# Weight pages that begin at another place of a 128-byte line in each stage

## The chip, the cores and the metric

The kernel runs on one core of one Trainium2 chip. The metric is the device time of one execution in microseconds (us). The time before is the median of three runs, 1609.99 us, and they lie between 1606.26 and 1611.5 us.

## The reference, cut to what matters

One layer of an encoder block on a sequence of 1024 tokens with 1024 channels, all in float32. Nearly all of the arithmetic is matrix products with the weights:

```python
h = rms_norm(h_res, norm_w[layer])
z = jnp.einsum('bsd,dc->bsc', h, w_in[layer])            # 1024 x 1024 by 1024 x 12288
qkv_a, g_a, q_b, zf_fwd, zf_bwd, i_b, g_b, zgate_a, zgate_b = jnp.split(z, split_points, axis=-1)
...                                                      # banded attention, 3 groups of 8 heads
y_a = (o_a * silu(g_a)) @ w_proj_a                       # 512 x 1024
...                                                      # gated linear recurrence, 8 heads, two directions
y_b = o_b @ w_proj_b                                     # 1024 x 1024
merged = sigmoid(zgate_a) * y_a + sigmoid(zgate_b) * y_b
h_res = h_res + merged @ w_out                           # 1024 x 1024
```

## The kernel before, in words

A product in float32 is made of three products in the faster type float32r: each operand x is split into a rounded part and a remainder (names with `hi` and `lo`, `sh` and `sl`, `mh` and `ml`), and hi·hi, hi·lo and lo·hi are summed in PSUM. So each step of a large product is three matmuls, and each of them has a 128x128 operand that is loaded into the array first (the stationary one) and a 128x512 operand that streams through it (the moving one). 5520 matmuls have this size.

The weights come as pages of 128x512 (2048 bytes in each partition). `feed` loads a raw page, `split` writes its rounded part into a tile `whi` (ScalarE) and the remainder into a tile `wlo` (GpSimd, for 16 pages VectorE). Both come from rings of 9 tiles, `hir` and `lor`, and `free_to` gives the tiles back once the products of a page have been issued. All pages are numbered in the order in which they are used; `split_next` is the number of the page that is split next, `b.w[n]` holds the two tiles of page n.

The normed input h stands transposed in SBUF for most of the run, in the tiles `hhi` and `hlo`. There are two kinds of product with it:

- `tok_group`: the weight page is moving, 128 tokens of h are stationary. Values, queries and keys of the attention, and i and g of the recurrence (called ig below) are made so. In the attention groups 1 and 2 the tokens are taken with a stride.
- `T_group`: a 128x128 part of the weight page is stationary, 512 tokens of h are moving. The gates and the q, f and f-backward columns of the recurrence are made so.

`run_unit` runs a group: 8 steps of three matmuls, 24 matmuls, into one PSUM bank `gp`. `run_quads` makes most of the gate columns with seven products for eight (tiles `qA`, `qC`, `qE`, sums of h in the tiles S0 to S3).

The order of the work is decided while the program is built, by a planner (`Plan`, `Builder`) with modelled times: `tick` and `burst` place the smaller tasks (splits, evacuations, and the small float32 matmuls of attention and recurrence) between the large groups. Rings of tiles with a fixed count decide how far ahead a task may run: `qq_ring` holds the evacuated q of the recurrence, `ld` the branch outputs that are loaded back from HBM before the output projections (`split_load`, then `split_store` into `sh` and `sl`).

The stages in order, with the large matmuls in each: u and V0 (values of group 0; 192), qk0 (384), values and qk of groups 1 and 2 with strided tokens (1152), ga (gate of branch A; 192), ig (four parts of 192), quads (504), the eight recurrence heads (144 each), sg (the last gates; 192), ya (projection of branch A; 192), yb (branch B; 384), out (output projection; 384). Small float32 matmuls run between the large ones nearly everywhere from qk0 to the last head.

Where the tiles lie, counted in bytes from the start of a 128-byte line: in the program before, `whi`, `wlo`, `hhi`, `hlo`, the sums S0 to S3 and the tiles of branch B in yb all begin at 96. The tiles of the attention and of the recurrence, `uhi` and `ulo` (the stationary operands of u), the tiles `sh` and `sl` of branch A (moving in ya) and `mh` and `ml` (stationary in out) begin at 32. The pages follow each other at 2048 bytes.

Of the kernel before, what the change touches and what calls it, by code (L numbers as in the profile page):

```python
# [8 lines left out]
F32 = mybir.dt.float32  # L9
F32R = mybir.dt.float32r  # L10
# [199 lines left out]
class Builder:  # L210
# [89 lines left out]
    def setup_weights(self, items, pool, ring, raws):  # L300
        self.RING = ring
        self.wpages, self.windex, self.quads, self.steps = [], [], [], []
        n = 0
        for k, it in enumerate(items):
            if not isinstance(it, tuple):
                self.wpages.append(it)
                self.windex.append(n)
                n += 1
                continue
            m = len(self.quads)  # L310
            self.quads.append(it)
            more = k + 1 < len(items) and isinstance(items[k + 1], tuple)
            if k == 0 or not isinstance(items[k - 1], tuple):
                self.steps.append((n, m, "11"))
                n += 1
            for op in ("T1", "T2", "21", "T3", "+", "22", "T4"):
                if op != "+":
                    self.steps.append((n, m, op))
                    n += 1
                elif more:  # L320
                    self.steps.append((n, m + 1, "11"))
                    n += 1
        self.ops = n
        self.w = {}
        self.rawr = self.ring(pool, "raw", raws, [128, 512])
        self.hir = self.ring(pool, "whi", ring, [128, 512], F32R)
        self.lor = self.ring(pool, "wlo", ring, [128, 512], F32R)
        self.raws = []
        self.raw_next = 0
        self.split_next = 0  # L330
        self.freed = 0
        self.offered = None
        self.scales = {}
# [17 lines left out]
            self.offer(t, k)  # L351

    def split(self, raw):
        hi, lo = self.hir.get(), self.lor.get()
        scale = self.scales.get(self.split_next)
        if scale is None:
            self.p.act.activation(hi, raw, AF.Copy)
            self.p.pool.tensor_tensor(lo, raw, hi.bitcast(F32), op=OP.subtract)
        else:
            self.p.act.activation(hi, raw, AF.Copy, scale=scale)  # L360
            self.p.dve.scalar_tensor_tensor(lo, raw, scale, hi.bitcast(F32), op0=OP.mult, op1=OP.subtract)
        self.w[self.split_next] = (hi, lo)
        self.split_next += 1
# [10 lines left out]

    def free_to(self, n):
        for i in range(self.freed, n):
            hi, lo = self.w.pop(i)
            self.hir.done(hi)
            self.lor.done(lo)
        self.freed = max(self.freed, n)  # L380
# [184 lines left out]
def hybrid_block(ctx, tc, a, out):  # L565
    b = Builder(ctx, tc, a)
    a_, v_, g_, t_, s_ = b.p.act, b.p.dve, b.p.pool, b.p.pe, b.p.sp
    consts = ctx.enter_context(tc.tile_pool(name="consts", bufs=1))
    wpool = ctx.enter_context(tc.tile_pool(name="wts", bufs=1))
    stg = ctx.enter_context(tc.tile_pool(name="stg", bufs=3))  # L570
    tiny = ctx.enter_context(tc.tile_pool(name="tiny", bufs=2))
# [31 lines left out]
    blocks = [(0, j) for j in range(0, 8, 2)] + [(1, j) for j in range(0, TAIL, 2)]  # L603
# [7 lines left out]
        items += gate_pages(1, j)  # L611
    items += [wpa[i] for i in range(8)] + [wpb[i] for i in range(16)] + [wo[i] for i in range(16)]
    b.setup_weights(items, wpool, RING, RAWS)


    nw = consts.tile([128, 8], F32, name="nw")
# [694 lines left out]
    hp = bctx.enter_context(tc.tile_pool(name="hgrn", bufs=1))  # L1311
# [25 lines left out]

    ig_ring = b.ring(hp, "ig", 8, [128, 512])
    sk_ring = b.ring(hp, "sk", 5, [128, 512])
    qq_ring = b.ring(hp, "q", 3, [128, 512])  # L1340
    lf_ring = b.ring(hp, "lf", 4, [128, 512])
    q2_ring = b.ring(hp, "q2", 4, [128, 4, 64])
    km_ring = b.ring(hp, "km", 4, [128, 512])
# [307 lines left out]
    ectx = {}  # L1651

    def end_start():
        bctx.close()
        ectx["ep"] = ep = ctx.enter_context(tc.tile_pool(name="end", bufs=1))
        ectx["ld"] = b.ring(ep, "ld", 6, [128, 512])
        for k in range(8):
            b.task("sp", [oaD], lambda k=k: split_load(OA, k % 4, k // 4, oaD[k % 4, k // 4],
                                                       lambda n: ep.tile([128, 512], F32R, tag="L", name=n, bufs=17)),
                   4, ectx["ld"].soon)  # L1660

    def split_load(to, j, half, src, new):
        t = ectx["ld"].get()
        s_.dma_start(t, src)
        b.task("act", [t], lambda: split_store(to, j, half, t, new), 4)
# [9 lines left out]
    for j in range(TAIL, 8):  # L1675
        for half in range(2):
            b.run_unit([T_group(pos, half, evac_sg(1, j, half), half == 1)])
            if not ectx and all(st.get("f", 0) == 2 for st in H.values()):
                end_start()
        pos += 2  # L1680
    b.drain()
    if not ectx:
        end_start()
        b.drain()
# [6 lines left out]
    ep = ectx["ep"]  # L1691
    ob = ctx.enter_context(tc.tile_pool(name="endo", bufs=1, side="right"))
    MA, MH, ML = {}, {}, {}
    for half in range(2):
        for h in range(8):
            k = 8 * half + h
# [39 lines left out]
    k = 0  # L1736
# [137 lines left out]
def _build(arrays):  # L1874
    import concourse.bacc as _bacc
    nc = _bacc.Bacc("TRN2", target_bir_lowering=False, num_devices=1)
    args = {n: nc.dram_tensor(f"in_{n}_dram", v.shape, mybir.dt.from_np(v.dtype), kind="ExternalInput").ap()
            for n, v in arrays.items()}
    out = nc.dram_tensor("out_0_dram", (S, D), F32, kind="ExternalOutput").ap()
    with tile.TileContext(nc) as tc:  # L1880
        hybrid_block(tc, args, out)
    return nc
# [9 lines left out]
```

## Time and profile before

| what | value |
|---|---|
| median of the runs | 1609.99 us (1606.26 to 1611.5) |
| the profiled execution | 1608.46 us, its span 1606.6 us |
| granted TensorE clock, mean | 0.99 |
| TensorE busy | 1569.1 us, 98% of the span |
| VectorE, ScalarE, GpSimd busy | 845.3, 659.5, 468.0 us |
| DMA | 148.31 MB, mean 92 GB/s |

TensorE is the engine to look at: it is busy nearly all of the span, the others half of it or less. A busy TensorE still says little about its pace, since matmuls overlap and their recorded ends are modelled. The pace is read from the start times of matmuls that follow each other, in the order of time; that distance is called the spacing below.

### The profile page before, as it was taken

What the parts mean: (1) busy time and instruction counts of PE and PEld (TensorE: products, weight loads), DVE (VectorE), ACT (ScalarE), POOL (GpSimd) and SP (SyncE); (2) the same over time, 40 slices, a digit from 0 to 9 for tenths busy, and PEclk for the clock granted to TensorE, in tenths of its full rate; (3) what the DMA queues carried; (4) which work ended last, traced back from release to release, by engine and by line L of the source; (5) the groups of instructions that cost most, each with busy time, mean ns of one, the idle gap of its engine ahead of it and who ended that gap; (6) DMA issues with size and microseconds to landing.
All of it is one profiled execution on the core that took longest, in us unless ns stands there. A gap on an engine that the chain in (4) does not pass through costs nothing. (4 is left out here: it accounts for less than half of the span.)

```text
span 1606.6 us, 23188 instructions
## 1 busy us (share of the span) xinstructions
PE 1569.1 (98%) x8373; PEld 1335.8 (83%) x8373; DVE 845.3 (53%) x2216; ACT 659.5 (41%) x1434; POOL 468.0 (29%) x462
## 2 busy tenths in 40 slices
PE   8899999999999999999899999999999999999999
PEld 6688899999999987678788888888877878888887
DVE  5667632575136642336412207988889887543211
ACT  5533542434334363213334437655565554422110
POOL 3411202202022031228434434433344423003320
PEclk9999999999999999899999999999999999999999
DMA  6402203102022035473413251121221211842232
GB/s 215 139 22 98 70 18 112 50 33 67 21 63 66 16 103 138 125 219 112 144 66 115 83 166 40 53 93 40 54 86 47 94 39 65 293 140 92 88 119 89
DMA packets 110879, 148.31 MB, mean 92 GB/s; under 512 B 24625, under 2 KB 48300, under 8 KB 110764
## 3 DMA queue, kind: packets, MB, share of 16 engines
q1 hardware_dynamic: 103340, 146.38, 29.1%
q8 instruction: 66, 1.08, 0.3%
q10 hardware_dynamic: 7424, 0.45, 0.3%
q14 instruction: 49, 0.40, 0.1%
HBM read 110.77 MB, written 40.73 MB: 94 GB/s over the span
## 5 line engine op out<-in xcount | busy, mean ns | idle before, releaser
L55 POOL TENSOR_TENSOR wlo<-raw,whi 128x512 fp32r<-128x512 f32 x192 | 253.9, 1328 | 685.8 <-ACT whi L55 670.4
L55 PE MATMUL gp<-whi,hhi 128*128 128x512 f32 x792 | 328.5, 415 | 8.3 <-ACT stage L55 5.7
L55 PE MATMUL gp<-wlo,hhi 128*128 128x512 f32 x792 | 316.0, 399 | 1.4 <-POOL wlo L55 1.4
L55 PE MATMUL gp<-whi,hlo 128*128 128x512 f32 x792 | 316.1, 399 | 0.0
L55 PEld LDWEIGHTS gp<-whi,hhi 128*128 128x128 f32 x792 | 200.5, 253 | 36.8 <-issue 10.0
L55 PEld LDWEIGHTS gp<-wlo,hhi 128*128 128x128 f32 x792 | 201.4, 254 | 18.3 <-POOL wlo L55 2.6
L55 PEld LDWEIGHTS gp<-whi,hlo 128*128 128x128 f32 x792 | 200.9, 254 | 17.9 <-DVE hlo L55 1.0
L55 PE MATMUL gp<-hhi,whi 128*128 128x512 f32 x512 | 209.4, 409 | 0.0
L55 PE MATMUL gp<-hhi,wlo 128*128 128x512 f32 x512 | 200.9, 392 | 0.0
L55 PE MATMUL gp<-hlo,whi 128*128 128x512 f32 x512 | 200.0, 391 | 0.0
L55 ACT ACTIVATE whi<-raw 128x512 fp32r<-128x512 f32 x192 | 119.3, 626 | 140.9 <-PE gp L55 81.7
L55 PEld LDWEIGHTS gp<-hhi,wlo 128*128 128x128 f32 x512 | 96.2, 188 | 21.3
L55 PEld LDWEIGHTS gp<-hhi,whi 128*128 128x128 f32 x512 | 96.8, 189 | 18.8 <-issue 1.0
L55 PEld LDWEIGHTS gp<-hlo,whi 128*128 128x128 f32 x512 | 96.8, 189 | 17.2
L55 ACT ACTIVATE s<-s,neg 128x192 f32<-128x192 f32 (+2 forms) x192 | 83.9, 439 | 65.5 <-DVE neg L55 65.3
L55 DVE TENSOR_REDUCE ss<-sq 128x8 f32<-128x512 f32 x48 | 32.8, 684 | 146.7 <-ACT sq L55 146.7
L55 POOL TENSOR_TENSOR wlo<-qraw,whi 128x512 fp32r<-128x512 f32 x42 | 55.0, 1316 | 76.9 <-ACT whi L55 76.7
L55 PE MATMUL gp<-sh,whi 128*128 128x512 f32 x192 | 75.0, 391 | 0.0
L55 PE MATMUL gp<-sh,wlo 128*128 128x512 f32 x192 | 74.9, 390 | 0.0
L55 PE MATMUL gp<-sl,whi 128*128 128x512 f32 x192 | 74.6, 389 | 0.0
L55 ACT ACTIVATE sq<-gp 128x512 f32<-128x512 f32 x48 | 28.0, 592 | 111.8 <-PE gp L55 91.4
L55 ACT ACTIVATE stage<-gp 128x512 f32<-128x512 f32 x48 | 28.0, 594 | 111.5 <-PE gp L55 88.3
(225 smaller groups left out, 2787.9 us busy)
## 6 DMA issues: line engine op xcount, KB each, us to landing
raw<-in_w_in_dram SPq DMA_DIRECT2D x168, 256.0 KB
igD<-stage SPq DMA_DIRECT2D x32, 256.0 KB
ig<-igD SPq DMA_DIRECT2D x32, 256.0 KB
sgl<-sgD SPq DMA_DIRECT2D x32, 256.0 KB
oD<-os SPq DMA_DIRECT2D x48, 128.0 KB
og<-oD SPq DMA_DIRECT2D x24, 256.0 KB
qraw<-in_w_in_dram SPq DMA_DIRECT2D x24, 256.0 KB
sgD<-spare SPq DMA_DIRECT2D x24, 256.0 KB
```

What stands on the lines that cost most here:

```text
L55: got = f(*args, **kw)
```

## The change

Each page is split into a tile that is 32 elements (128 bytes) longer than the page, and begins at a place in it that a table `place` gives for the page's number. Two small tiles that nothing uses are put in front, so that the tiles begin at 64 within a line; with the table's offsets the places are 68, 72, 80, 88, 92, 100, 104, 112, 120 and 0, and 96 for pages that the table does not name. To make room in SBUF, `qq_ring` has 2 tiles instead of 3 and `ld` 5 instead of 6.

```diff
-        self.hir = self.ring(pool, "whi", ring, [128, 512], F32R)
-        self.lor = self.ring(pool, "wlo", ring, [128, 512], F32R)
+        self.hir = self.ring(pool, "whi", ring, [128, 544], F32R)
+        self.lor = self.ring(pool, "wlo", ring, [128, 544], F32R)
+        self.wt = {}
+        self.place = {}
...
     def split(self, raw):
-        hi, lo = self.hir.get(), self.lor.get()
+        self.wt[self.split_next] = self.hir.get(), self.lor.get()
+        o = self.place.get(self.split_next, 96)
+        o = (o - 64) // 4 if o else 16
+        hi, lo = (t[:, o:o + 512] for t in self.wt[self.split_next])
...
+    consts.tile([128, 8], F32, name="lowPad")
+    consts.tile([128, 16], F32, name="lowPad2")
...
+    first = 112 + 7 * len(blocks)
+    spans = [(8, 16, 104), (16, 24, 112), (80, 88, 120), (88, 96, 0), (96, 104, 88), (104, 112, 80), (72, 80, 92)]
+    spans += [(first + 6 * h, first + 6 * h + 6, o) for h, o in enumerate((104, 112, 120, 0, 88, 80, 72, 100))]
+    spans += [(first + 48, first + 56, 68)]
+    for lo, hi, o in spans:
+        b.place.update({k: o for k in range(lo, hi)})
...
-    qq_ring = b.ring(hp, "q", 3, [128, 512])
+    qq_ring = b.ring(hp, "q", 2, [128, 512])
...
-        ectx["ld"] = b.ring(ep, "ld", 6, [128, 512])
+        ectx["ld"] = b.ring(ep, "ld", 5, [128, 512])
```

By stage, with the weight page moving or stationary, and h (the other operand) at 96:

| stage | large matmuls | the weights are | their place |
|---|---|---|---|
| qk0, first half, second half | 192, 192 | moving | 104, 112 |
| ga | 192 | stationary | 92 |
| ig, parts 1 to 4 | 192 each | moving | 120, 0, 88, 80 |
| heads 0 to 7 | 144 each | stationary | 104, 112, 120, 0, 88, 80, 72, 100 |
| sg | 192 | stationary | 68 |

All others keep 96. The two small tiles in front move every other tile of that side of SBUF as well: in the program after, what began at 32 begins at 0 (the tiles of attention and recurrence, `uhi` and `ulo`, `sh` and `sl` of branch A, `mh` and `ml`), and what began at 64 begins at 32. The other side, with h, S0 to S3 and the tiles of branch B, stays at 96. The pages now follow each other at 2176 bytes, 17 lines.

TensorE's instructions stand in the same order as before, and so do GpSimd's. On SyncE, which issues the loads, the shorter ring moves one load of branch A behind a load of a weight page (`raw`) and a store of a gate (`sgD`), at the start of ya. Before:

```order
L55 DMA ld_13001<-oaD 128x512
L55 DMA ld_13003<-oaD 128x512
L55 DMA ld_13005<-oaD 128x512
L55 DMA ld_13007<-oaD 128x512
L55 DMA ld_13009<-oaD 128x512
L55 DMA ld_13011<-oaD 128x512
L55 DMA raw_13019<-in_w_proj_b_dram 128x512
L55 DMA sgD<-stage_13041 128x512
L55 DMA ld_13044<-oaD 128x512
L55 DMA ld_13046<-oaD 128x512
```

On SyncE at the same place after the change:

```order
L55 DMA ld_13003<-oaD 128x512
L55 DMA ld_13005<-oaD 128x512
L55 DMA ld_13007<-oaD 128x512
L55 DMA ld_13009<-oaD 128x512
L55 DMA ld_13011<-oaD 128x512
L55 DMA raw_13019<-in_w_proj_b_dram 128x512
L55 DMA sgD<-stage_13041 128x512
L55 DMA ld_13044<-oaD 128x512
L55 DMA ld_13046<-oaD 128x512
L55 DMA ld_13059<-oaD 128x512
```

Five loads instead of six stand ahead of the page, and three instead of two behind the store. Later in ya some of the 16 loads of branch B trade places with loads of gates in the same way, and with them a few of the ScalarE and VectorE instructions that split them.

On ScalarE the ring of q adds a wait for VectorE in heads 2, 4 and 6, where the first q of the head is evacuated. `on`, `km` and `qr` are tiles of the recurrence too. Before, in head 2:

```order
L55 ACTIVATE on_9819<-oB_9807 128x512 [waits PE_49]
L55 ACTIVATE q_9827<-gp_9777 128x512 [waits PE_49]
L55 ACTIVATE km_9850<-lf_9721 128x4x64 [waits DVE_49,Activation_49,Pool_49]
L55 ACTIVATE km_9850<-q_8_9799 128x4x64 [waits DVE_49]
L55 ACTIVATE qr_9853<-lf_9721 128x512
```

On ScalarE at the same place after the change:

```order
L55 ACTIVATE on_9821<-oB_9809 128x512 [waits PE_49]
L55 ACTIVATE q_9829<-gp_9779 128x512 [waits DVE_49,PE_49]
L55 ACTIVATE km_9852<-lf_9723 128x4x64 [waits DVE_49,Activation_49,Pool_49]
L55 ACTIVATE km_9852<-q_8_9801 128x4x64 [waits DVE_49]
L55 ACTIVATE qr_9855<-lf_9723 128x512
```

The row of q has `DVE_49` among its waits, and nothing else moved there.

More of the change, by code (lines that the diff above doesn't have):

```diff
@@ L376, in free_to @@
         for i in range(self.freed, n):
-            hi, lo = self.w.pop(i)
+            self.w.pop(i)
+            hi, lo = self.wt.pop(i)
             self.hir.done(hi)
```

## The prediction

> **What bounds the kernel now.** I read the page first, for the engine and the chain that ended last.
>
> ```profile
> PE 1569.1 (98%) x8373; PEld 1335.8 (83%) x8373; DVE 845.3 (53%) x2216; ACT 659.5 (41%) x1434; POOL 468.0 (29%) x462
> ...
> 1369.90 232.96 PE gp L55 x1014
> ```
>
> TensorE (PE) is busy for 98% of the span, and the chain that ended last is, for its final 233 us, nothing but large matmuls one behind the other. So the time is set by the pace of matmuls that never wait, and a change of their operands' places acts on the end directly. That pace is the spacing of starts, from the order of time. Three stages run without a break, so their first and last start and their count give it. First the fourth part of ig (192 matmuls, from 785.69 to the first matmul after it), then ya (192, from 1382.04 to 1426.00), then out (383 spacings, from 1513.09 to 1602.46):
>
> ```profile
> 785.69 0.39 PE L55 MATMUL gp<-whi,hhi 128*128 128x512 f32 x1
> 829.21 0.39 PE L55 MATMUL qA<-hhi,whi 128*128 128x512 f32 x1
> ...
> 1382.04 0.40 PE L55 MATMUL gp<-sh,whi 128*128 128x512 f32 x1
> 1426.00 0.40 PE L55 MATMUL gp<-sh,whi 128*128 128x512 f32 x1
> ...
> 1513.09 0.40 PE L55 MATMUL gp<-whi,mh 128*128 128x512 f32 x1
> 1602.46 0.39 PE L55 MATMUL gp<-whi,ml 128*128 128x512 f32 x1
> ```
>
> ig: 43.52 us / 192 = 226.7 ns. ya: 43.96 / 192 = 229.0 ns. out: 89.37 / 383 = 233.3 ns. The matmuls have one shape and type, the clock is full, no other instruction lies between. What differs is where the operands begin in a 128-byte line: both at 96 in ig, moving at 32 and stationary at 96 in ya, moving at 96 and stationary at 32 in out. So places do matter, by up to 6.7 ns, and the equal pair 96/96 is the fastest of the three.
>
> Where small matmuls interrupt the large ones, the spacing needs time to settle. After such a break in ga:
>
> ```profile
> 579.24 0.40 PE L55 MATMUL gp<-hlo,whi 128*128 128x512 f32 x1
> ...
> 579.94 0.39 PE L55 MATMUL gp<-hlo,whi 128*128 128x512 f32 x1
> 580.16 0.39 PE L55 MATMUL gp<-hhi,wlo 128*128 128x512 f32 x1
> ...
> 581.55 0.39 PE L55 MATMUL gp<-hhi,wlo 128*128 128x512 f32 x1
> 582.23 0.39 PE L55 MATMUL gp<-hhi,wlo 128*128 128x512 f32 x1
> ```
>
> Ten spacings, 579.24 to 581.55, take 2.31 us, 231 ns each, though every operand stands at 96; the next three, to 582.23, take 0.68 us, 227 ns. The same pair has thus a slower, unsettled pace and a settled one, and single spacings between are as short as 0.22 us (579.94 to 580.16).
>
> **The change part by part.** It moves 2688 large matmuls to another place: qk0 384, ga 192, ig 768, the heads 1152, sg 192. Nothing is added to TensorE, and nothing moves there. Not all of these spacings are free to change: ig (768) and head 0 (144) run nearly all settled, the other 1776 stand among small matmuls, and of a group of 24 about ten recover as above and one or two hold the break. I count half of them, 888. That makes 1800 spacings whose settled value the new place decides.
>
> No row shows the new pairs. The bounds from rows: above, out's 233.3 ns, 6.7 ns over the present 226.7; below, the shortest single spacing seen, 0.22 us, 6.7 ns under it. Times 1800 that is +12.1 us and -12.1 us. For the value I weigh two readings. If the spacing grows evenly with the distance between the two places, the nearest rows are ya and out, both 64 bytes apart, at 229.0 and 233.3, mean 231.2, 4.5 ns over. The new distances are 4 to 32 bytes, 17 on average over the moved matmuls, which gives 4.5 x 17/64 = 1.2 ns. If instead 96/96 is special and any other pair stays at an unsettled pace, the price is 231 - 226.7 = 4.3 ns. I take the middle, 2.8 ns, since the two rows at 64 lie on both sides of that pace: 1800 x 2.8 ns = +5.0 us.
>
> A second reading of the same three numbers is worth having: 226.7 and 233.3 are 34 and 35 times 6.67 ns, and 229.0 is 34 and a third. The spacing seems to snap to steps. Then single stages will stay exactly at 226.7, or go to 233.3, or lie at a fraction, and the sum is a mean over the stages; the 2.8 ns is that mean, not the price of each.
>
> The two pads move operands of stages that keep 96. In out (384) the stationary operand goes from 32 to 0: from 64 bytes apart to 32. Half way between 226.7 and 233.3 is 230.0, so 384 x -3.3 ns = -1.3 us, with ends -2.6 (226.7) and 0. In u (about 80 free spacings, the same pair) -0.3. In ya the moving operand goes from 32 to 0, again from 64 to 32 apart; its 229.0 lies between the other two already, so 0, with ends -0.4 (226.7) and +0.8 (233.3). The small matmuls have both operands moved by the same 32 bytes, so I cost them at nothing; were that wrong, the cover would be none, since they lie on TensorE's path.
>
> [...]
>
> The shorter rings. The first q of heads 2, 4 and 6 now waits until the head before has used its q up. The last use by head 1 and the first q of head 2:
>
> ```profile
> 1046.67 0.68 DVE L55 TENSOR_TENSOR qr<-qr,q 128x512 f32<-128x512 f32 x1
> ...
> 1062.68 0.60 ACT L55 ACTIVATE q<-gp 128x512 f32<-128x512 f32 x1 [0.78 <-PE gp L55]
> ```
>
> The tile is free at 1047.4 and wanted at 1062.7: 15 us of cover, cost 0. Behind that ScalarE instruction stand the exponentials of the neighbouring head, which would be late if the cover went. Of `ld`, the sixth load of branch A now waits for the first tile, and stands behind a page and a store:
>
> ```profile
> 1378.54 2.06 DVE L55 TENSOR_TENSOR sl<-ld,sh 128x512 fp32r<-128x512 f32 x3 [0.71 <-ACT sh L55]
> ...
> 1384.19 1.28 DVE L55 TENSOR_TENSOR sl<-ld,sh 128x512 fp32r<-128x512 f32 x2
> ...
> 1413.07 0.68 DVE L55 TENSOR_TENSOR sl<-ld,sh 128x512 fp32r<-128x512 f32 x1
> ```
>
> Before, branch A's last two tiles are ready at 1385.5. A group of ya has four steps, 12 matmuls; the second starts 12 spacings after 1382.04, at 1384.8, and needs the last tile nine spacings on, at 1386.9. The eighth load now waits for the third tile's split, which ended at about 1379.9, and could come some 1 to 2 us later than before against a cover of 1.4 us: I cost it at 0, at most 1 us once, and the second group of ya would show it. Branch B's last split ends at 1413.8 and yb begins at 1426.0, 12 us of cover. SyncE's loads of pages behind it are taken in by the raw ring.
>
> Sum: +5.0 - 1.3 - 0.3 = +3.4 us on the profiled execution's 1608.5, 1611.9. That execution is 1.5 us under the median, 1610.0, so I predict 1613.4. A difference under 0.3%, 4.8 us, is about what a measurement of this kernel cannot tell from none.
>
> **The rivals.** *Slower by more:* most new pairs lock at the pace of out. Its place is the settled part of ig and the heads; +12.1 us, with out unchanged, gives 1622. It decides from a mean price of 3.6 ns on (1800 x 3.6 = 6.5 us, less 1.6, is 4.9), a mean spacing of 230.3. For it: two of the three pairs seen are slower, and 96/96 is the only one that settles at 34 steps. A second sign: ya and out are both 64 bytes apart and differ by 4.3 ns, so the distance within a line is not all that counts; pages at 17 lines now alternate between even and odd lines, and if that matters quads and yb (888 matmuls at 226.7 now) lose too, half of them up to 6.7 ns, 3 us. Against it: most new pairs are nearer to each other than 64.
>
> *Faster:* equal places are no good place for two streams that start together, and some new ones settle below 226.7. It decides from -1.8 ns, 224.9 (1800 x -1.8 = -3.2 us, less 1.6, is -4.8). At the lower bound 1610 - 12.1 - 2.9 = 1595; half way, about 1602. For it: single spacings of 0.22 us occur. Against it: no stage holds one, and both other pairs seen are slower.
>
> *Nothing happens:* the places of these pairs make no difference, as between equal pairs, and only noise is left: 1610. [...] For it: if the spacing snaps to steps, a small shift may leave a stage on its step. Against it: it would have to hold for ten places at once.
>
> **How the numbers follow.** Forecast (a small loss inside 0.3%) 0.34, nothing happens 0.07, a loss over 0.3% 0.40 of which about half in the neighbourhood of the forecast and half towards 1622, faster 0.19. So faster 0.19, same 0.41, slower 0.40. The forecast's own range is 1608 to 1616. The range given reaches up to 1623, the upper rival with its time, and down to 1602, the middle of the lower one; beyond are about 2 in 10.
>
> **What would show it.** The starts of the large matmuls, stage by stage: the four parts of ig one by one, head 0, and after each break whether the spacing comes back to 226.7. I expect them between 226.7 and 233.3, unequal among the places, with a mean near 229.5; out under 233.3; quads and yb still at 226.7; no new wait of TensorE at the start of ya or in heads 2, 4 and 6. The prediction is wrong if the places change nothing, if most stages lock at 233 or above, or if any of them settles near 220.

## The result, and the profile after

The change makes the kernel slower: 1621.14 us median (1620.77 to 1622.49) against 1609.7 us of the kernel before, a ratio of 1.0075 with a 95% interval of 1.0057 to 1.0093. The time lies inside the range given, near its upper end. It is the value of the rival "slower by more" (1622), not of the forecast (1613.4).

The page of the kernel after, with its profiled execution of 1622.49 us, and the last and longest piece of its chain of work:

```profile
span 1620.7 us, 23188 instructions
...
PE 1588.1 (98%) x8373; PEld 1340.7 (83%) x8373; DVE 835.6 (52%) x2216; ACT 659.9 (41%) x1434; POOL 457.3 (28%) x462
```

```profile
1380.84 236.08 PE gp L55 x1014
```

The span grew by 14.1 us, with the same 8373 matmuls and TensorE still busy for 98% of it. The same 1014 matmuls at the end of the chain take 236.08 us instead of 232.96. So the time went into the pace of the matmuls, which the order of time gives. First one row of before that the prediction did not need, the first matmul after the quads, then the rows of after: the fourth part of ig, the quads, the first head, ya, yb and the two ends of out.

```profile
943.45 0.39 PE L55 MATMUL gp<-hhi,whi 128*128 128x512 f32 x1
```

```profile
789.85 0.39 PE L55 MATMUL gp<-whi,hhi 128*128 128x512 f32 x1
...
833.98 0.39 PE L55 MATMUL qA<-hhi,whi 128*128 128x512 f32 x1
...
951.33 0.40 PE L55 MATMUL gp<-hhi,whi 128*128 128x512 f32 x1
...
1393.04 0.40 PE L55 MATMUL gp<-sh,whi 128*128 128x512 f32 x1
...
1437.74 0.40 PE L55 MATMUL gp<-sh,whi 128*128 128x512 f32 x1
...
1527.13 0.40 PE L55 MATMUL gp<-whi,mh 128*128 128x512 f32 x1
...
1616.50 0.40 PE L55 MATMUL gp<-whi,ml 128*128 128x512 f32 x1
```

The quads take 117.35 us for 504 matmuls, 232.8 ns each, against 114.24 us (943.45 less 829.21) or 226.7 before. Yb takes 89.39 us for 384, 232.8 against 226.8. Neither stage has a page in the table of places: both keep 96. Together they lose 3.11 + 2.30 = 5.4 us, nearly half of the loss. The fourth part of ig, whose page did move (to 80), has 44.13 / 192 = 229.8; ya went from 229.0 to 232.8; out stays at 233.3.

Not all of the pace reached the span. The waits of TensorE, first the three longest of before, then the same three after (engine and product, what it waited for, us in total, times, longest):

```profile
PE gp L55 <- ACT stage L55: 5.7, 1, 5.7
PE U L55 <- ACT kT L55: 5.5, 4, 2.6
PE oB L55 <- DVE S L55: 5.4, 4, 3.2
```

```profile
PE oB L55 <- DVE S L55: 5.0, 4, 3.1
...
PE U L55 <- ACT kT L55: 4.2, 3, 2.0
...
PE gp L55 <- ACT stage L55: 3.7, 1, 3.7
```

All rows of that view add up to 33.6 us before and 28.7 after, 4.9 us less, most of it in ig and in the heads. One reading, the author's own estimate, is that slower matmuls leave the other engines more time, so that part of the loss in pace fills time that was waited before. No run shows it apart, since GpSimd also became faster. Its remainders of the pages, before and after (count, busy us, mean ns):

```profile
L55 POOL TENSOR_TENSOR wlo<-raw,whi 128x512 fp32r<-128x512 f32 x192 | 253.9, 1328 | 685.8 <-ACT whi L55 670.4 <-PE kT L55 4.8 <-PE U L55 3.3
```

```profile
L55 POOL TENSOR_TENSOR wlo<-raw,whi 128x512 fp32r<-128x512 f32 x192 | 241.7, 1265 | 701.1 <-ACT whi L55 685.2 <-PE kT L55 4.9 <-PE U L55 4.7
```

Sorted by the place of the page, the median is 1094 ns for the 62 pages at 68, 72, 88, 100, 104 and 120, and 1292 for the 130 at 0, 80, 92, 96 and 112. The run with the places alone (below) has the same two medians.

### The profile page after: what moved, and what is told of

Read it like the earlier page. It is cut to its first block, busy times and chain, and to the rows that moved or that the text cites. A ratio compares the mean times of both kernels' runs of the same rounds, so it can differ in the third digit from the quotient of the medians.

```text
span 1620.7 us, 23188 instructions
## 1 busy us (share of the span) xinstructions
PE 1588.1 (98%) x8373; PEld 1340.7 (83%) x8373; DVE 835.6 (52%) x2216; ACT 659.9 (41%) x1434; POOL 457.3 (28%) x462
## 5 line engine op out<-in xcount | busy, mean ns | idle before, releaser
L55 POOL TENSOR_TENSOR wlo<-raw,whi 128x512 fp32r<-128x512 f32 x192 | 241.7, 1265 | 701.1 <-ACT whi L55 685.2
```

The costliest lines, as they stand in the source:

```text
L55: got = f(*args, **kw)
```

## Experiments

Two columns of numbers run through all of them: the time, and the mean spacing by stage. The second is worked out from all start times in ns, over the spacings under 262 ns (longer ones hold small matmuls or a wait). "Moved" are the stages that the table of places names, some 2400 such spacings; "strided" is 1070, quads 504, ya 192, yb 384, out 383.

| kernel | span, us | moved | strided | quads | ya | yb | out |
|---|---|---|---|---|---|---|---|
| before | 1606.6 | 227.9 | 240.0 | 226.7 | 229.0 | 226.8 | 233.3 |
| after | 1620.7 | 231.9 | 241.0 | 232.8 | 232.8 | 232.8 | 233.3 |
| pitch alone | 1622.6 | 231.5 | 240.8 | 232.6 | 232.2 | 232.7 | 231.4 |
| rings alone | 1609.7 | 227.8 | 240.0 | 226.7 | 229.0 | 226.8 | 233.3 |
| places alone | 1612.7 | 232.1 | 239.9 | 226.7 | 228.9 | 226.8 | 233.3 |
| all pages 128 further | 1626.5 | 232.6 | 242.3 | 232.4 | 228.9 | 232.4 | 233.3 |
| u, ya, out at the pages' place | 1606.8 | 227.9 | 239.9 | 226.7 | 226.7 | 226.7 | 226.7 |

Three theories stood against each other. A: what counts is the distance of the moving from the stationary operand within 256 bytes, two lines, and pages at 17 lines stand 128 bytes further off every other time. B: the ten places make the loss. C: the shorter rings do.

### The pitch alone

```diff
-        self.hir = self.ring(pool, "whi", ring, [128, 512], F32R)
-        self.lor = self.ring(pool, "wlo", ring, [128, 512], F32R)
+        self.hir = self.ring(pool, "whi", ring, [128, 544], F32R)
+        self.lor = self.ring(pool, "wlo", ring, [128, 544], F32R)
...
+        hi, lo = (t[:, 0:512] for t in self.wt[self.split_next])
```

> Only the page pitch of 2176 bytes (17 lines) and the shorter rings are kept; all pages begin at 96 and nothing else moves. Theory A (what counts is the distance of moving and stationary operand within two lines, 256 bytes, and an odd pitch puts half of the pages 128 bytes further from h): quads and yb show 232 to 234 ns as after the change, and so do qk0, ga, ig, the heads and sg, which stood at 227 to 229; some 3500 spacings by 4 to 6 ns is +14 to +20 us, so 1620 to 1630, or 1617 where unsettled stretches lose less. Theory B (the ten places make the loss): 1610, quads and yb at 226.7. Theory C (the shorter rings): +11 us in new waits, no spacing changed.

Measured: 1624.58 us, ratio 1.0086 (1.0061 to 1.0111). This one edit costs as much as the whole change; the intervals of the two ratios overlap, so which of them is slower is not decided. Its order of time, with the same first rows of stages (ig's fourth part, quads, first head, yb, out, and the end of out):

```profile
788.94 0.39 PE L55 MATMUL gp<-whi,hhi 128*128 128x512 f32 x1
...
833.21 0.39 PE L55 MATMUL qA<-hhi,whi 128*128 128x512 f32 x1
...
950.43 0.39 PE L55 MATMUL gp<-hhi,whi 128*128 128x512 f32 x1
...
1440.41 0.39 PE L55 MATMUL gp<-sh,whi 128*128 128x512 f32 x1
...
1529.77 0.39 PE L55 MATMUL gp<-whi,mh 128*128 128x512 f32 x1
...
1618.39 0.39 PE L55 MATMUL gp<-whi,ml 128*128 128x512 f32 x1
```

Every page begins at 96 here, as before, and yet quads go at 117.22 / 504 = 232.6 ns, yb at 89.36 / 384 = 232.7, ig's fourth part at 44.27 / 192 = 230.6. The place within a line is thus not enough to tell the pace. Theory A had expected 232 to 234 of the moved stages too; those with moving pages stay under it (ig's fourth part), those with stationary pages come to 231.8 (ga) to 232.5 (sg). Out gains a little (88.62 / 383 = 231.4).

### The rings alone

Only `qq_ring` with 2 tiles and `ld` with 5.

> Only the two shorter rings; pages, places and pitch as before. Theories A and B: 1610, within 3 us, all spacings as before. Theory C: 1621, with waits of TensorE in heads 2, 4 and 6 or at the start of ya.

Measured: 1611.02 us, ratio 1.0005 (0.9994 to 1.0016): no difference. Quads, first and next stage:

```profile
829.71 0.39 PE L55 MATMUL qA<-hhi,whi 128*128 128x512 f32 x1
...
943.95 0.39 PE L55 MATMUL gp<-hhi,whi 128*128 128x512 f32 x1
```

114.24 us, as before, and all rows of the waits of TensorE add up to 33.7 us, as before. C is out. Its span is nevertheless 3.1 us longer than that of before, one profiled execution against another. These lines are stretches around the last head, of before, of this kernel and of the kernel after (from:to, length, busy time of PE, PEld, DVE, ACT, POOL, then the granted clock, DMA share and GB/s):

```profile
1272.00:1324.00 52.00, 48.14 (x307) 40.78 (x306) 44.86 (x97) 29.80 (x56) 19.36 (x24) 1.00 0.14 42
```

```profile
1273.00:1327.00 54.00, 50.13 (x303) 42.79 (x303) 44.41 (x97) 29.53 (x54) 19.42 (x24) 0.94 0.13 40
```

```profile
1280.00:1335.00 55.00, 51.43 (x307) 43.41 (x306) 42.42 (x97) 29.88 (x55) 18.41 (x24) 0.94 0.14 40
```

By the starts of its matmuls the last head takes 54.0 us here and 51.3 before, with a granted clock of 0.94 instead of 1.00. The kernel after has 0.94 there too. So two or three microseconds between these two single profiles (2.7 in the last head) come with where the clock dips, and a comparison of spacings stage by stage is sharper than one of spans.

### The places alone

To keep all pages on the same half of 256 bytes with the same memory, both parts of a page share a tile of 34 lines, 2048 bytes apart.

```diff
+        self.pair = self.ring(pool, "w", ring, [128, 1088], F32R)
...
+        o = self.place.get(self.split_next, 0) // 4
+        hi, lo = t[:, o:o + 512], t[:, o + 512:o + 1024]
```

> The ten places with an even pitch: rounded part and remainder of a page lie in one tile of 4352 bytes (34 lines), 2048 bytes apart, so that every page stands 4 to 32 bytes from h within two lines, and none 128 further; shorter rings, no pads. Theory A: quads and yb back at 226.7, the moved stages between 226.7 and 230, 1610 to 1614. Theory B: 1620, the moved stages at 232 to 233 as after the change. Theory C: 1621 with every spacing as before.

Measured: 1614.21 us, ratio 1.0025 (1.0014 to 1.0035). Ig's fourth part, the quads, the first head:

```profile
786.78 0.39 PE L55 MATMUL gp<-w,hhi 128*128 128x512 f32 x1
...
831.59 0.39 PE L55 MATMUL qA<-hhi,w 128*128 128x512 f32 x1
...
945.85 0.40 PE L55 MATMUL gp<-hhi,w 128*128 128x512 f32 x1
```

Quads are back at 114.26 / 504 = 226.7 ns: their loss was the pitch. These pages follow each other at 17 times 256 bytes, so their distance from h modulo 512 is now 0 and now 256; a period longer than 256 bytes does not show. The moved stages did not behave as theory A expected of small distances: 44.81 / 192 = 233.4 in ig's fourth part (16 bytes off), 232.1 on the mean. Against the run with the rings alone that is 4.3 ns on some 2400 spacings, 10.3 us. Of it only 3.0 us stand in the span (1612.7 against 1609.7). The waits of TensorE show where most of the rest went:

```profile
PE oB L55 <- DVE S L55: 5.1, 4, 3.1
PE U L55 <- ACT kT L55: 4.7, 3, 2.2
...
PE gp L55 <- ACT stage L55: 3.8, 1, 3.8
```

All rows add up to 29.5 us, 4.2 less than with the rings alone. For the last 3 us there is the granted clock, first of the rings alone, then of this kernel:

```profile
core 0: 1609.7 us, clock 0.987
```

```profile
core 0: 1612.7 us, clock 0.990
```

It is so in every run: 0.986 to 0.989 in ten runs of the rings alone, 0.990 to 0.992 in ten of the places alone. The difference of the means, 0.0025, is 4 us of 1610 (an estimate). Why the clock is higher here stays open, and so does what the shorter waits are due to: the pitch alone, with moved stages as slow, has 32.2 us of waits, and the kernel with all pages 128 further 31.8. Only the two kernels with places that make GpSimd faster are under 30.

### All pages 128 bytes further, in the kernel before

```diff
+    consts.tile([128, 32], F32, name="lowPad")
```

> The kernel before with one unused tile of 128 bytes in front, so that all tiles of that side, the pages too, stand 128 bytes further; each keeps its place in a line and the pitch stays 2048. Theory A: every product of a page with h, the sums or branch B is 128 bytes apart in two lines, as the slowest mix in quads after the change, 235 ns where it was 226.7 (3600 spacings by 7 ns or a little less: +20 to +27 us, 1630 to 1637); u, ya and out, where both operands move together, stay at 233.3, 229.0 and 233.3. Theory B: nothing changes within a line, 1610.

Measured: 1625.46 us, ratio 1.0101 (1.0078 to 1.0124). Ig's fourth part, quads, first head, ya, yb:

```profile
792.57 0.39 PE L55 MATMUL gp<-whi,hhi 128*128 128x512 f32 x1
...
837.18 0.39 PE L55 MATMUL qA<-hhi,whi 128*128 128x512 f32 x1
...
954.30 0.39 PE L55 MATMUL gp<-hhi,whi 128*128 128x512 f32 x1
...
1399.73 0.40 PE L55 MATMUL gp<-sh,whi 128*128 128x512 f32 x1
...
1443.68 0.40 PE L55 MATMUL gp<-sh,whi 128*128 128x512 f32 x1
```

One unused tile, one line long, costs 1%: no place within a line, no ring, no pitch and no order of instructions differs from before. Ig has 44.61 / 192 = 232.3 ns, quads 117.12 / 504 = 232.4. Ya, whose two operands moved together, keeps its 43.95 / 192 = 228.9. The distance within 256 bytes sets the pace here (quads 226.7 ns at 0, 232.4 at 128), and 128 is not worse than most others (228.4 to 234.5 in the table further down): the expected 235 and with it the expected 1630 to 1637 were too high, since 235 had been read from stretches in which the distance changes.

### The slow stages at the pages' place

If distance is the cause, u, ya and out were slow before for the same reason, and can be cured.

```diff
+    pre.tile([128, 48], F32, name="prePad")
...
+        ep.tile([128, 48], F32, name="endPad")
```

> The kernel before, pages as they were; two unused tiles of 192 bytes move the stationary operands of u and out and the moving one of ya to the pages' own place within two lines (distance 0 instead of 192, 192 and 64). Nothing else moves. Theory A (the distance within two lines sets the spacing): out 233.3 to 226.7 ns, 383 x 6.7 = -2.6 us; ya 229.0 to 226.7, -0.4 us; u -0.5 us: 1606.5, ratio 0.998. A rival, that these stages are slow for another reason than the distance (they read what was written shortly before): no spacing changes, 1610.

Measured: 1606.01 us, ratio 0.9976 (0.9965 to 0.9986), the fastest version of this study, with an order of instructions equal to before on every engine. First of ya, of yb, and both ends of out:

```profile
1385.19 0.39 PE L55 MATMUL gp<-sh,whi 128*128 128x512 f32 x1
...
1428.71 0.39 PE L55 MATMUL gp<-sh,whi 128*128 128x512 f32 x1
...
1515.75 0.39 PE L55 MATMUL gp<-whi,mh 128*128 128x512 f32 x1
...
1602.57 0.39 PE L55 MATMUL gp<-whi,ml 128*128 128x512 f32 x1
```

Out: 86.82 / 383 = 226.7 ns instead of 233.3, 2.55 us less; ya 43.52 / 192 = 226.7 instead of 229.0, 0.44 less. The span in the table shows no gain, since this profiled execution had a granted clock of 0.987 and that of before 0.990; the spacings and the median do. The rival, that these stages were slow because of what was written just before, falls.

### Position or distance

```diff
+    consts.tile([128, 56], F32, name="lowPad")
...
+    rpool = ctx.enter_context(tc.tile_pool(name="rp", bufs=1, side="right"))
+    rpool.tile([128, 8], F32, name="highPad")
```

> The kernel before with all tiles of one side 224 bytes higher and of the other 32 bytes lower, so that pages, h, sums and branch B stand at a multiple of 64 bytes (192 within two lines) instead of 224, still at distance 0 from each other. If only the distance counts (theory A in its narrow form): every spacing as before, 1610. Rival: the position itself counts as well, a start off a 64-byte boundary costs a step of 6.7 ns: the settled 226.7 becomes 220, some 3000 spacings, 1590.

Measured: 1610.61 us, ratio 1.0003 (0.9993 to 1.0014). Ig's fourth part, quads, first head:

```profile
784.84 0.39 PE L55 MATMUL gp<-whi,hhi 128*128 128x512 f32 x1
...
828.36 0.39 PE L55 MATMUL qA<-hhi,whi 128*128 128x512 f32 x1
...
942.60 0.39 PE L55 MATMUL gp<-hhi,whi 128*128 128x512 f32 x1
```

43.52 / 192 and 114.24 / 504 are 226.7 both. At distance 0 the position itself does not count here; a start on a multiple of 64 bytes gains nothing.

### A map of distances

With the shared tiles, the short rings and no pads, each stage got its distance from the table `place`.

> A map of distances: pages in tiles that hold both parts, with a place per stage in steps of 16 bytes over two lines (V0 64, qk0 64 and 192, ga 64, ig 96, 160, 208, 48, heads 96, 160, 192, 224, 48, 208, 112, 144, sg 176, the strided stages 64, 192, 32, 64, 192, 224), u, ya and out at 0. Theory A: u, ya, out and yb at 226.7; every other stage locks at a fixed value between 228 and 236, none below 226.7; the total 1620 to 1632. Rival: the distance matters only when it is small or 128 and others are as good as 0: half of the stages at 226.7, 1612.

Measured, one run: 1614.6 us, under what theory A expected (1620 to 1632) and nearer to the rival's 1612; TensorE's waits are 2.4 us shorter than with the rings alone (31.3), and the granted clock is higher, 0.991. The spacings have to decide. Ig's fourth part (48 bytes off), the quads, and both ends of out (0):

```profile
790.70 0.40 PE L55 MATMUL gp<-w,hhi 128*128 128x512 f32 x1
...
835.50 0.39 PE L55 MATMUL qA<-hhi,w 128*128 128x512 f32 x1
...
1521.76 0.39 PE L55 MATMUL gp<-w,mh 128*128 128x512 f32 x1
...
1608.62 0.39 PE L55 MATMUL gp<-w,ml 128*128 128x512 f32 x1
```

44.80 / 192 = 233.3, and 86.86 / 383 = 226.8. From this run, the one with the places alone, the one with all pages 128 further and before, the settled pace (mean spacing from the eleventh of a stretch on) by the distance, moving less stationary, modulo 256:

| distance | settled pace, ns |
|---|---|
| 0 (both at 32, at 192 or at 224 of 256) | 226.7 |
| 64 (pages moving; stationary) | 228.9; 228.9 |
| 96 (pages moving; stationary) | 233.3; 233.3 |
| 128 (pages moving; stationary) | 232.6; 232.6 |
| 160 (pages moving; stationary) | 234.3; 234.3 |
| 192 (pages moving; stationary) | 233.3; 233.4 |
| 4, 8, 28, 32, 48, 80, 112, 144, 224, 232, 240, 248, 252 | 230.1 to 233.3 |
| 24 (pages moving; stationary) | 234.5; 231.1 |
| 16 (pages moving; stationary) | 231.7; 228.4 |
| 208 (pages moving; stationary) | 230.7; 233.3 |

No distance tried is below 226.7, and none but 0 reaches it, so the rival (only small distances and 128 matter) falls. For most distances seen both ways it is the same within about 0.5 ns whichever operand the page is; 16, 24 and 208 are exceptions, by 2.6 to 3.4 ns, that stay unexplained. The paces between 228.4 and 234.5 are no steps of 6.7 ns.

### Why pages that alternate lose as much

In the pitch run a matmul of quads is 128 off only half of the time, and still they are at 232.6, the pace of 128 throughout. Two runs take apart what alternates there. In the first, remainders stand 128 bytes off and rounded parts at 0, in all pages:

```diff
-        hi, lo = t[:, o:o + 512], t[:, o + 512:o + 1024]
+        hi, lo = t[:, o:o + 512], t[:, o + 544:o + 1056]
```

> Why pages that alternate lose nearly as much as pages that all stand 128 bytes off. Here every rounded part stands at distance 0 from h and every remainder at 128, the same in all pages (even pitch, shorter rings): of three matmuls in a row two are at 0 and one at 128. If each matmul pays by its own distance alone: quads and the fourth part of ig at 226.7 + 5.7/3 = 228.6 ns, 1616. If a change of distance from one matmul to the next costs, as an unsettled stretch does: 231 to 233 ns, 1621 to 1625.

In the second, both parts of every odd page stand 128 bytes off:

```diff
+    b.place = {k: 128 * (k % 2) for k in range(b.ops)}
```

> Here both parts of a page stand at the same distance, 0 in pages of even number and 128 in pages of odd number: the distance changes with the page, not within three matmuls. If each matmul pays by its own distance alone: 229.5 ns in quads and the fourth part of ig, 1618 to 1620. If each change costs a new settling of some ten spacings at 231: quads changes every 12 matmuls and ig every three, so quads near 230 to 231, ig 231 to 233, 1620 to 1625.

Measured, one run each: 1624.36 and 1619.25 us. Quads, first and next stage, of the first and of the second:

```profile
834.72 0.40 PE L55 MATMUL qA<-hhi,w 128*128 128x512 f32 x1
...
951.21 0.39 PE L55 MATMUL gp<-hhi,w 128*128 128x512 f32 x1
```

```profile
831.47 0.39 PE L55 MATMUL qA<-hhi,w 128*128 128x512 f32 x1
...
948.07 0.40 PE L55 MATMUL gp<-hhi,w 128*128 128x512 f32 x1
```

116.49 / 504 = 231.1 ns and 116.60 / 504 = 231.3. The time of the second lies where "by its own distance alone" had it (1618 to 1620), but its quads are not at 229.5; one run with its clock and waits does not decide that, the spacings do. Single spacings of quads in ns tell more. In the first run quads repeat three values: 226.7 where the matmul and the one after it are both at 0; 232.5 where its own distance is 0 but the next stationary operand, which is loaded meanwhile (in the quads of before such a load takes 188 ns and begins within 4 ns of the matmul ahead of it), is the remainder 128 off; 234.1 where it is the remainder itself and the next is at 0. So one operand off spoils two spacings of three: in these quads, where the pages are stationary, a matmul pays for its own operand (234.1) and for the next one (232.5). In the second run the twelve matmuls of an odd page have a mean of 233.0, and those of an even page do not come back at once (means by their position in the page): 236, 224, 231, 236, 228, 232, 231, then four of 227, and 232 at the change, a mean of 229.8. The same values, 236, 224, 231, 236, 228, 232, 231 and then 227, stand in the break in ga that the prediction shows (579.71 to 581.32), so the two are read as one and the same recovery. "Each matmul pays by its own distance alone" falls in both runs. For moving pages the first run has no such rule: the four parts of ig have the same distances there (0, 128, 0) and a mean of 230.7, 232.5, 232.9 and 231.1, which stays open.

## Why the prediction was right or wrong

- **What bounds the kernel.** Right: the pace of matmuls that never wait sets the time, operands' places set the pace (226.7 ns in ig, 229.0 in ya, 233.3 in out, with a granted clock of 1.00 in all three stretches), and the pair at distance 0 is the fastest (226.7). The settled values were indeed unequal, between 226.7 and 234.5, and none lay near 220; they do not snap to steps of 6.67 ns. The lower bound of 220 came from rows rounded to 10 ns: the spacing from 579.94 to 580.16 is 224 ns, one value of the recovery that has 236 on both sides.
- **The step that failed** is the sentence that nothing else changes: "quads and yb still at 226.7". The prediction took the place within a 128-byte line as what counts, and gave the other possibility, pages that alternate between even and odd lines, to the upper rival as "a second sign". That sign was what the runs bore out (quads at 232.6 ns with the pitch alone, 226.7 with the places alone). Quads, yb, ya and the strided stages, none of them in the table, lost 3.11 + 2.30 + 0.74 + 1.14 (1070 x 1.07 ns) = 7.3 us of pace (in ya the pads moved an operand as well; with the pitch alone it loses 0.6). The rival had put it at 3 us for quads and yb, half of them at 6.7 ns; nearly all of them went up, by 6.2 and 6.0.
- **The price of the new places**, 1800 x 2.8 ns = 5.0 us, was mis-sized in both factors. The places alone cost 4.3 ns on some 2400 spacings, 10.3 us. That is the price of the second of the two readings weighed, and not the even growth with distance. Its reason, that any other pair stays at one unsettled pace of 231, does not hold: the settled paces there run from 228.4 to 234.5. Nor did the stretches among small matmuls shelter half of theirs.
- **A term was missing:** the waits of TensorE shrink. In the run with the places alone they lost 4.2 us, after the change 4.9, with the pitch alone 1.5. The +5.0 us for the places is near the 3.2 us measured for them over the rings alone (1614.21 less 1611.02), but by luck: 10.3 us of pace stand against shorter waits and a higher clock.
- **In the changed kernel places and pitch do not add.** Moved stages stand at 232.1 with the places alone, 231.5 with the pitch alone, 231.9 with both. So on the stages the forecast looked at, either edit would have done the same, and the pitch does the rest: 9.6 (2405 x 4.0 ns) + 7.3 = 16.9 us of pace, less 4.9 of waits, is 12.0. The span grew by 14.1; for the missing 2.1 there is the granted clock, 0.988 in the mean against 0.990 before (the last head alone took 3.0 us longer, only 0.5 of it pace). That the time came out at the rival's 1622 is luck as well: the rival had 12.1 us from 1800 moved spacings, the runs show 9.6 from 2405, 7.3 from others and fewer waits.
- **The pads:** out was to gain 1.3 us and gained none (233.3). With the odd pitch its distance alternates between 224 and 96, and these settle at 233.2 and 233.3 where a stage has one of them alone.
- **The rings** at 0: right, 1.0005 (0.9994 to 1.0016). The third tile's split in the sum of the cover ended at 1379.2, not at 1379.9 (that is the fourth's), which changes nothing.
- **What stays open.** The line of 128 bytes in front cost 1.0101 (1.0078 to 1.0124), and with it quads went from 226.7 to 232.4 ns. The runs show that the loss follows the distance of TensorE's two operands; why it does is not shown.

## What to carry to other kernels

Where TensorE is busy throughout, read the spacing of starts stage by stage, and compare it with where the program puts the moving and the stationary operand modulo 256 bytes; give both the same remainder, by a pad in a pool (here 192 bytes took out from 233.3 to 226.7 ns). A tile that is widened, or a small tile put in front, shifts everything behind it: an odd number of lines changed the pace of stages that the edit does not name (quads from 226.7 to 232.4 ns with one line in front). And before a gain or a loss in pace is multiplied out, look for waits in the same stage, since they can take part of it (TensorE's fell from 33.6 to 28.7 us here), and compare the granted clock of the two profiles (0.990 and 0.988 here).

## What the runs showed of the hardware

- The pace of the float32r matmuls of 128x512 in these kernels, each with a new stationary operand, followed the distance of the operands modulo 256 bytes, not 128: 226.7 ns at 0 and 232.6 at 128. At 0 it was the same at three positions (226.7 at 32, 192 and 224), so the distance counts, and pages 0 and 256 off modulo 512 have it alike (226.7 in quads with the places alone).
- Of the distances tried 0 alone had the best pace, 226.7 ns, the others 228.4 to 234.5, and there was no slope: 4 bytes off cost 5.8 ns (232.5), 64 bytes 2.3.
- The stationary operand of the following matmul counted too, in the quads of the run with the remainders 128 off (232.5 ns at distance 0 with the next one 128 off, 226.7 with the next one at 0).
- After twelve matmuls at distance 128 (quads with the odd pages 128 off), or after a break with small matmuls (ga before), the pace of 227 ns came back only after about seven spacings (236 to 224 ns). It was not so after every change: behind a single matmul 128 off, in the quads with the remainders 128 off, 226.7 ns stood at once.
- GpSimd's subtraction of a 128x512 page took 1094 ns in the median where the page began at 68, 72, 88, 100, 104 or 120 of a line, and 1292 at 0, 80, 92, 96 or 112. Why is not shown.
